# Data work of the gate-and-up and down products taken from GpSimd to VectorE in a hybrid encoder trunk

## The chip, the core and the metric

The kernel runs on one core of one Trainium2 chip. The metric is the device time of one execution in microseconds, of which the median over several executions counts.

## The reference, cut to what matters

The model is an encoder trunk of two layers on 1040 tokens (16 learned tokens ahead of 1024) of width 1024. What the change touches is the second half of each layer, the feed-forward network, and the norm ahead of it:

```python
for l in range(DEPTH):                       # DEPTH = 2
    h = h + hybrid_mixer(rmsnorm(h, norm1_w[l]), ...)   # ends in mix @ w_out
    h = h + swiglu(rmsnorm(h, norm2_w[l]), w_gate_up[l], w_down[l])
h = rmsnorm(h, final_norm_w)

def rmsnorm(x, w):
    y = x * lax.rsqrt(jnp.mean(x * x, axis=-1, keepdims=True) + RMS_EPS)
    return y * w

def swiglu(h, w_gate_up, w_down):            # 1024 -> 2 x 2816 -> 1024
    gate, up = jnp.split(h @ w_gate_up, 2, axis=-1)
    return (jax.nn.silu(gate) * up) @ w_down
```

All data is float32.

## The kernel before, in words

Activations lie transposed: 128 features on the partitions, tokens along the free dimension. Every float32 operand of a product is split into a high part (rounded to the type that TensorE takes, by a copy on ScalarE) and a low part (operand minus high part), and a product is three matmuls: high times high, high times low, low times high. So each weight tile of 128 x 512 costs one copy on ScalarE and one subtraction, and the subtraction is what most of the change moves.

The work of a layer, in order of the parts that matter here:

- **Output projection** (`out_part`, called twice for each of the 8 feature blocks, `z` naming the half of the tokens). Its weights come through `wload` and `wsplit`; their low parts are made on GpSimd (L131) and stay there. After each block, ScalarE squares the new residual (L949) and L950 adds it to the running sum of squares. For `z == 1` and even `m` above 0 that addition is on GpSimd, three times in a layer.
- **Operands of gate and up.** Gate and up are computed together by a scheme of seven products P1 to P7 on 2 x 2 blocks instead of eight (Strassen's idea: blocks of tokens, of input features, and the pair gate/up). The token operands B11, B21, B22, T1 to T4 are sums of normalised blocks, formed on VectorE in L1078, L977, L178 and L965 while the last blocks of the output projection still run. In this stretch the weights A11 and A12 of the first four feature rows are already multiplied (`early_part`, eight calls of `w_op`).
- **Gate and up**, a loop over `f`, 22 rows of 128 features. For each row four weight tiles are loaded (A11, A12, A21, A22), four sums are formed on VectorE (L1290, L1291, L1294, L1295), seven tiles (five for the first four rows) are split by `w_op` (high part L997 on ScalarE, low part L998), and seven products run, in layer 0 in two parts `j` of 260 columns, in layer 1 in one part of 512. VectorE and ScalarE read the products out of PSUM (P5 at L1314, P6 and P3 at L1325 and L1328, P7 at L1332, P4 at L1341; P1 and P2 on ScalarE). P3 is accumulated into the bank of P5, P7 and P4 into the bank of P6, so these products wait until the product before them in their bank has been read out. At the end of a row gate and up are multiplied by the scale of the norm (gate L1355, up L1356), gate goes through SiLU on ScalarE (L1357), and L1358 multiplies the two.
- **Down**, 84 units (`UNITS`) of the same scheme on w_down: `w_unit` splits one weight tile of 128 x 384 (high part L1196, low part L1197), five units ahead of its use; `t_pair` splits the token operand (L1244, L1245). `behind(...)` adds an order dependency on the read-out of two units before.

`tt` is an elementwise operation of two tensors on VectorE, `ptt` the same on GpSimd, `act` an operation on ScalarE. The order of the instructions in each engine's queue is not written out by hand: a scheduler places them by its own cost model, so a change of engine also changes the orders of the queues. Each engine works through its queue in order.

Of the kernel before, what the change touches and what calls it, by code (L numbers as in the profile page):

```python
# [7 lines left out]
F32 = mybir.dt.float32  # L8
# [3 lines left out]
ALU = mybir.AluOpType  # L12
# [30 lines left out]
def trunk(ctx: ExitStack, tc: tile.TileContext, xT, w_in, w_ba, w_out, w_gu, w_dn,  # L43
# [8 lines left out]
    def nm(p):  # L52
        cnt[0] += 1
        return f"{p}_{cnt[0]}"
# [45 lines left out]
    tt = nc.vector.tensor_tensor  # L100
    stt = nc.vector.scalar_tensor_tensor
    ts = nc.vector.tensor_scalar
    ptt = nc.gpsimd.tensor_tensor
# [42 lines left out]
    def dense(ws, xs, chunks, evac, pool=None):  # L146

        for (n0, n1) in chunks:
            n = n1 - n0
            ps = (pool or pacc)()  # L150
            K = len(xs)
            here = tc.cur_priority
            if mmp[0] is not None:
                at_prio(mmp[0])
            for k in range(K):
                (wh, wl), (xh, xl) = ws[k], xs[k]
                mm(ps[:, :n], wh, xh[:, n0:n1], start=(k == 0), stop=False)  # L157
                mm(ps[:, :n], wh, xl[:, n0:n1], start=False, stop=False)  # L158
                mm(ps[:, :n], wl, xh[:, n0:n1], start=False, stop=(k == K - 1))  # L159
            if mmp[0] is not None:  # L160
                mmp[0] = tc.cur_priority
                at_prio(here)
            here = tc.cur_priority
            if evp[0] is not None:
                at_prio(evp[0])
            evac(ps[:, :n], n0, n1)
            if evp[0] is not None:
                evp[0] = tc.cur_priority
                at_prio(here)
            for q in (jobs, jobs2, jobs3):  # L170
                f = q.pop(0) if q else None
                if f is not None:
                    f()
# [106 lines left out]
    for l in range(DEPTH):  # L280
# [660 lines left out]
        def out_part(z, m):  # L941
            dense(wload(w_out[l, m, :, 0:4, :], 4), os_, hcut[z], add_h(m), pwide)

            v, sv = half(hr[m][:, o0:L], z), half(ss[:, o0:L], z)
            if m == 0:
                act(out=sv, in_=v, func=AF.Square)
            else:
                sq = c4k("sq")[:, 0:NB].rearrange("p (g e) -> p g e", g=2)
                act(out=sq, in_=v, func=AF.Square)  # L949
                (ptt if z == 1 and m % 2 == 0 else tt)(out=sv, in0=sv, in1=sq, op=ALU.add)  # L950
            for (n0, n1) in hcut[z]:
                dma(hd[m][:, n0:n1], hr[m][:, n0:n1])

# [39 lines left out]
        def w_op(src, early=False):  # L993
            hi, lo = wslot(early)
            n = src.shape[1]
            hi, lo = hi[:, 0:n, :], lo[:, 0:n, :]
            act(out=hi, in_=src, func=AF.Copy)  # L997
            ptt(out=lo, in0=src, in1=hi.bitcast(F32), op=ALU.subtract)  # L998
            return hi, lo

        bn = [0]
# [116 lines left out]
        def behind(ins):  # L1118

            return after(ins, read_out.get(at[0] - 2))  # L1120
# [58 lines left out]
        def w_unit(u):  # L1179

            p, b, m = UNITS[u]
            n = 4 * b + m
            i = u % 8
            if i in (0, 4, 6):
                hi, lo = (wp.tile([128, WK, 128], F32R, tag=t, name=nm(t)).rearrange("p a b -> p (a b)")[:, 0:384] for t in ("whi", "wlo"))
            else:
                j = {1: 0, 2: 1, 3: 2, 5: 3, 7: 4}[i]
                hi, lo = (dw["W"][:, 384 * (2 * j + q):384 * (2 * j + q) + 384] for q in range(2))
            if p in ("P5", "P6", "P7"):
                r = s_raw(n)  # L1190
            elif p == "P3":
                r = a_raw(0, 1, n)
                behind(tt(out=r, in0=r, in1=s_raw(n), op=ALU.subtract))
            else:
                r = a_raw(*{"P2": (0, 1), "P1": (0, 0), "P4": (1, 1)}[p], n)
            act(out=hi, in_=r, func=AF.Copy)  # L1196
            ptt(out=lo, in0=r, in1=hi.bitcast(F32), op=ALU.subtract)  # L1197
            dw["w", u] = [t.rearrange("p (k e) -> p k e", k=3) for t in (hi, lo)]

        def t_raw(i):  # L1200
# [79 lines left out]
        for f in range(FT):  # L1280
            A11, A12, A21, A22 = raw4("raw"), raw4("raw"), raw4("ck2"), raw4("ck2")
            dma(A11, w_gu[l, f, 0, :, 0:4, :])
            dma(A21, w_gu[l, f, 1, :, 0:4, :])
            dma(A22, w_gu[l, f, 1, :, 4:8, :])
            dma(A12, w_gu[l, f, 0, :, 4:8, :])
            s1t, s2t = raw4("ck2"), raw4("ck2")
            W = {}
            if f >= NE:
                W["A11"] = w_op(A11)
            tt(out=s1t, in0=A21, in1=A22, op=ALU.add)  # L1290
            tt(out=s2t, in0=s1t, in1=A11, op=ALU.subtract)  # L1291
            W["S1"] = w_op(s1t)
            W["S2"] = w_op(s2t)
            tt(out=s2t, in0=A12, in1=s2t, op=ALU.subtract)  # L1294
            tt(out=A21, in0=A11, in1=A21, op=ALU.subtract)  # L1295
            end = f == FT - 1
            for n, a in ([("S3", A21), ("A22", A22), ("S4", s2t), ("A12", A12)] if end else
                         [("S4", s2t), ("S3", A21), ("A12", A12), ("A22", A22)]):
                if f >= NE or n != "A12":
                    W[n] = w_op(a)  # L1300
            adds = s_under(f)
            g, u = early[f] if f < NE else (row((X[1], Y[1])[f % 2] + "f"), row(X[1], F32, 3))
            ps = {}


            def p1(j):
                ps["a", j], ps["c", j], ps["b", j] = pbank(), pbank(), pbank()
                if f >= NE:
                    prod(ps["a", j], W["A11"], T["B11"], j, True)
                    act(out=part(u, 0, j), in_=pin(ps["a", j]), func=AF.Copy)  # L1310

            def p5(j):
                prod(ps["c", j], W["S1"], T["T1"], j, True)
                tt(out=part(u, 1, j), in0=pin(ps["c", j]), in1=part(u, 0, j), op=ALU.add)  # L1314

            def p3(j):
                prod(ps["c", j], W["S4"], T["B22"], j, False)
                (gadd if end else gset)(ps["c", j], j)

            def p6(j):  # L1320
                prod(ps["b", j], W["S2"], T["T2"], j, True)
                (gset if end else gadd)(ps["b", j], j)

            def gset(p, j):
                tt(out=part(g, 1, j), in0=pin(p), in1=part(u, 0, j), op=ALU.add)  # L1325

            def gadd(p, j):
                tt(out=part(g, 1, j), in0=pin(p), in1=part(g, 1, j), op=ALU.add)  # L1328

            def p7(j):  # L1330
                prod(ps["b", j], W["S3"], T["T3"], j, False)
                tt(out=part(u, 1, j), in0=pin(ps["b", j]), in1=part(u, 1, j), op=ALU.add)  # L1332

            def p2(j):
                if f >= NE:
                    prod(ps["a", j], W["A12"], T["B21"], j, False)
                    act(out=part(g, 0, j), in_=pin(ps["a", j]), func=AF.Copy)

            def p4(j):
                prod(ps["b", j], W["A22"], T["T4"], j, False)  # L1340
                tt(out=part(u, 0, j), in0=pin(ps["b", j]), in1=part(u, 0, j), op=ALU.add)  # L1341

            p1_ = (p1, p6, p7)
            if end:

                for p in (p1, p5, p6, p7, p4, p3, p2):
                    for j in range(NJ):
                        p(j)
                    down_begins(p)
            else:  # L1350
                for j in range(NJ):
                    for p in (p1, p5, p3, p6, p7, p2, p4):
                        p(j)
            gv, uv, rv = g[:, o0:L], u[:, o0:L], ss[:, o0:L]
            ptt(out=gv, in0=gv, in1=rv, op=ALU.mult)  # L1355
            tt(out=uv, in0=uv, in1=rv, op=ALU.mult)  # L1356
            act(out=gv, in_=gv, func=AF.Silu)  # L1357
            row_done = tt(out=uv, in0=uv, in1=gv, op=ALU.mult)  # L1358
            for to, r, o in adds:
                after(tt(out=to, in0=r, in1=o, op=ALU.add), row_done if f < FT - 1 else row_before)  # L1360
            row_before = row_done
            dma(ad[f][:, o0:L], uv)
            if NF <= f < NF + NP:
                tt(out=gv[:, 0:NB].rearrange("p (g e) -> p g e", g=2), in0=half(uv, 1), in1=half(uv, 0), op=ALU.subtract)
                dma(td[f - NF], gv[:, 0:NB])
# [45 lines left out]
        for u, (p, b, m) in enumerate(UNITS):  # L1411
            if b == 1 and p in FIRST:
                dh, z = FIRST[p]
# [14 lines left out]
            for j in range(NJ):  # L1428
# [9 lines left out]
                if b == NBK - 1:  # L1438
                    dh, z, op = TO[p]
# [11 lines left out]
        else:  # L1451
# [22 lines left out]
            for (n0, n1) in FIN:  # L1474
                e = (n1 - n0) // 4
                sv = ss[:, n0:n1]
# [6 lines left out]
                for m in range(KT):  # L1483
# [4 lines left out]
                    else:  # L1488
                        summed(sv, True, False)
                        sq = c4k("sq")[:, 0:n1 - n0]  # L1490
# [87 lines left out]
```

## Time and profile before

| | |
|---|---|
| runs | 2550.4, 2552.06, 2552.34 us; median 2552.06 us |
| span of the profiled execution | 2550.9 us |
| TensorE (PE) busy | 2489.1 us, 98% of the span |
| VectorE (DVE) busy | 1636.6 us, 64% |
| GpSimd (POOL) busy | 1135.7 us, 45% |
| ScalarE (ACT) busy | 1045.7 us, 41% |
| mean granted TensorE clock | 0.996 of full speed |

The profile does not state the profiled execution's time apart from its span; the span lies among the three runs, 1.2 us below their median. In rows of the trace, a line such as L998 is a line of the kernel, followed by engine, operation, and written tile <- read tiles. In the table by windows each row is a stretch of the span: its length, then the busy time and number of instructions of each engine, the granted clock and the share and rate of the DMA engines. In the table of waits a row says which engine, tile and line waited for which, the total, the count and the longest wait.

Layer 0 has its output projection until about 625 us, gate and up from there to about 1070 us, and down to 1262 us; layer 1 has the same parts until about 1890, 2325 and 2500 us.

### The profile page before, as it was taken

The page shows a single profiled execution, that of the slowest core. Times are in us where ns is not written, and L with a number is a line of the kernel's source. Part 1 is how long each engine was busy: PE and PEld are TensorE (multiplying, and loading weights), DVE is VectorE, ACT ScalarE, POOL GpSimd, SP SyncE. Part 2 cuts the span into 40 slices and gives each one's busy share as a digit, 9 for nine tenths or more (in the row PEclk, how much of TensorE's full clock was granted, in tenths as well). Part 3 has the DMA queues.
Part 4 walks back from the last instruction along what each step waited for, and adds up shares of the span by engine and source line. Part 5 has one row for each costly group of instructions (what it writes and reads, how often), then busy time and mean ns, then how long its engine had stood idle before and what let it go on. Part 6 is the DMA issues. An engine that isn't in the chain of part 4 may idle for free. (4 is left out here: it accounts for less than half of the span.)

```text
span 2550.9 us, 45282 instructions
## 1 busy us (share of the span) xinstructions
PE 2489.1 (98%) x17508; PEld 2277.7 (89%) x17508; DVE 1636.6 (64%) x2547; ACT 1045.7 (41%) x1944; POOL 1135.7 (45%) x885
## 2 busy tenths in 40 slices
PE   8999999998999999999999999999989999999998
PEld 6989999998999999999999888998968778777787
DVE  4788233749766655767657892335687777558664
ACT  5554333535233333344445543334443333234444
POOL 2131212525666666655411212233557666575662
PEclk9999999999999999999999999999999999999999
DMA  3445253633223322764224443446332233328641
GB/s 129 135 158 169 100 167 125 202 93 119 97 101 103 108 92 85 236 204 136 92 81 144 148 159 108 156 129 201 121 118 91 95 107 103 100 94 273 189 121 66
DMA packets 199531, 335.27 MB, mean 131 GB/s; under 512 B 23404, under 2 KB 85668, under 8 KB 199316
## 3 DMA queue, kind: packets, MB, share of 16 engines
q1 hardware_dynamic: 171204, 293.84, 35.6%
q10 hardware_dynamic: 25936, 34.19, 4.1%
q0 software_dynamic: 2176, 4.36, 0.6%
q8 instruction: 137, 2.24, 0.4%
q14 instruction: 78, 0.64, 0.1%
HBM read 250.31 MB, written 81.99 MB: 130 GB/s over the span
## 5 line engine op out<-in xcount | busy, mean ns | idle before, releaser
L131 POOL TENSOR_TENSOR wlo<-raw,whi 128x512 fp32r<-128x512 f32 x132 | 177.7, 1348 | 661.2 <-ACT whi L130 538.0
L157 PE MATMUL pacc<-a,whi 128*128 128x346 f32 (+1 forms) x808 | 263.7, 329 | 8.0 <-ACT whi L130 7.7
L159 PE MATMUL pacc<-a,wlo 128*128 128x346 f32 (+1 forms) x808 | 262.3, 326 | 0.9 <-DVE wlo L131 0.5
L157 PE MATMUL pacc<-b,whi 128*128 128x346 f32 (+2 forms) x672 | 233.6, 348 | 2.5 <-ACT b L900 1.8
L159 PE MATMUL pacc<-b,wlo 128*128 128x346 f32 (+2 forms) x672 | 232.7, 348 | 0.8 <-DVE wlo L131 0.8
L158 PE MATMUL pacc<-a,whi 128*128 128x346 f32 (+1 forms) x688 | 224.9, 327 | 0.0
L158 PE MATMUL pacc<-b,whi 128*128 128x346 f32 (+2 forms) x580 | 200.3, 345 | 0.0
L130 ACT ACTIVATE whi<-raw 128x512 fp32r<-128x512 f32 x168 | 106.0, 631 | 224.1 <-PE pacc L158 119.0
L998 POOL TENSOR_TENSOR wlo<-rw,whi 128x512 fp32r<-128x512 f32 x92 | 133.8, 1456 | 74.8 <-ACT whi L997 73.5
L157 PEld LDWEIGHTS pacc<-a,whi 128*128 128x128 f32 x808 | 152.2, 189 | 13.8 <-ACT whi L130 8.1
L159 PEld LDWEIGHTS pacc<-a,wlo 128*128 128x128 f32 x808 | 152.6, 189 | 2.0 <-POOL wlo L131 0.7
L157 PEld LDWEIGHTS pacc<-b,whi 128*128 128x128 f32 x672 | 126.5, 188 | 14.4 <-issue 3.1
L159 PEld LDWEIGHTS pacc<-b,wlo 128*128 128x128 f32 x672 | 126.3, 188 | 9.7 <-DVE wlo L131 1.0
L158 PEld LDWEIGHTS pacc<-a,whi 128*128 128x128 f32 x688 | 130.0, 189 | 3.0 <-issue 1.9
L998 POOL TENSOR_TENSOR a<-rw,a 128x512 fp32r<-128x512 f32 x64 | 105.8, 1655 | 57.2 <-ACT a L997 56.2
L998 POOL TENSOR_TENSOR b<-rw,b 128x512 fp32r<-128x512 f32 x64 | 91.1, 1427 | 85.2 <-ACT b L997 59.8
L997 ACT ACTIVATE whi<-rw 128x512 fp32r<-128x512 f32 x92 | 57.8, 630 | 147.0 <-DVE rw L1294 76.7
L158 PEld LDWEIGHTS pacc<-b,whi 128*128 128x128 f32 x580 | 109.2, 188 | 7.0 <-issue 0.4
L997 ACT ACTIVATE b<-rw 128x512 fp32r<-128x512 f32 x64 | 40.1, 630 | 128.6 <-PE pacc L1016 32.3
L1290 DVE TENSOR_TENSOR rw<-rw,rw 128x512 f32<-128x512 f32 x44 | 61.4, 1395 | 45.6 <-POOL wlo L998 25.4
L296 DVE TENSOR_TENSOR a<-pacc,rstd 128x346 f32<-128x346 f32 (+2 forms) x59 | 32.6, 554 | 89.4 <-PE pacc L159 89.1
L998 POOL TENSOR_TENSOR wlo<-raw,whi 128x512 fp32r<-128x512 f32 x50 | 73.3, 1468 | 31.7 <-ACT whi L997 25.1
(967 smaller groups left out, 8439.8 us busy)
## 6 DMA issues: line engine op xcount, KB each, us to landing
raw<-in_w_in SPq DMA_DIRECT2D x112, 256.0 KB, 2.7
raw<-in_w_gu SPq DMA_DIRECT2D x104, 256.0 KB, 2.7
rw<-in_w_gu SPq DMA_DIRECT2D x88, 256.0 KB, 3.1
rw<-in_w_dn SPq DMA_DIRECT2D x94, 192.0 KB, 2.5
rec<-vkd SPq DMA_DIRECT2D x61, 256.0 KB, 2.8
raw<-in_w_out SPq DMA_DIRECT2D x48, 256.0 KB, 2.5
b<-ad SPq DMA_DIRECT2D x45, 260.0 KB, 3.4
a<-ad SPq DMA_DIRECT2D x45, 256.0 KB, 4.1
```

The costliest lines, as they stand in the source:

```text
L130: whi_done[0] = act(out=hi, in_=raw[:, 0:kk, :], func=AF.Copy)
L131: (tt if lov[0] else ptt)(out=lo, in0=raw[:, 0:kk, :], in1=hi.bitcast(F32), op=ALU.subtract)
L157: mm(ps[:, :n], wh, xh[:, n0:n1], start=(k == 0), stop=False)
L158: mm(ps[:, :n], wh, xl[:, n0:n1], start=False, stop=False)
L159: mm(ps[:, :n], wl, xh[:, n0:n1], start=False, stop=(k == K - 1))
L296: tt(out=t[:, n0:n1], in0=ps, in1=rstd[:, n0:n1], op=ALU.mult)
L997: act(out=hi, in_=src, func=AF.Copy)
L998: ptt(out=lo, in0=src, in1=hi.bitcast(F32), op=ALU.subtract)
L1290: tt(out=s1t, in0=A21, in1=A22, op=ALU.add)
```

## The change

Four expressions move from GpSimd to VectorE. No operand, shape or count changes. The low parts of `w_unit` also get the order dependency `behind`.

```diff
@@ out_part: sums of squares, three a layer
-                (ptt if z == 1 and m % 2 == 0 else tt)(out=sv, in0=sv, in1=sq, op=ALU.add)
+                tt(out=sv, in0=sv, in1=sq, op=ALU.add)
@@ w_op: low parts of the gate and up weights
-            ptt(out=lo, in0=src, in1=hi.bitcast(F32), op=ALU.subtract)
+            tt(out=lo, in0=src, in1=hi.bitcast(F32), op=ALU.subtract)
@@ w_unit: low parts of the down weights
-            ptt(out=lo, in0=r, in1=hi.bitcast(F32), op=ALU.subtract)
+            behind(tt(out=lo, in0=r, in1=hi.bitcast(F32), op=ALU.subtract))
@@ end of a row of gate and up: the norm's scale on gate
-            ptt(out=gv, in0=gv, in1=rv, op=ALU.mult)
+            tt(out=gv, in0=gv, in1=rv, op=ALU.mult)
```

`wsplit` (L131), the scale products of the mixer and the last norm's scaling keep their work on GpSimd.

## The prediction, made before the changed kernel ran

> **What bounds the kernel now.** I read the page first, then busy times by stage, then what TensorE waits for in each stage, then the rows of VectorE (DVE) and GpSimd (POOL) side by side at one of these waits.
>
> ```profile
> span 2550.9 us, 45282 instructions
> PE 2489.1 (98%) x17508; PEld 2277.7 (89%) x17508; DVE 1636.6 (64%) x2547; ACT 1045.7 (41%) x1944; POOL 1135.7 (45%) x885
> ```
>
> TensorE is busy for 2489.1 of 2550.9 us. No change on another engine can win more than the 61.8 us that it stands idle, and only the part of it that lies in the stages touched. The table by windows splits the two layers into ramp (last output projection, operands of gate and up), first rows, steady rows, and down:
>
> ```profile
> core 0: us, PE busy (x) PEld busy (x) DVE busy (x) ACT busy (x) POOL busy (x), PEclk, DMA share, GB/s
> 575.00:625.00 50.00, 43.64 (x348) 41.97 (x347) 47.81 (x53) 25.82 (x46) 26.59 (x17) 1.00 0.39 118
> 625.00:700.00 75.00, 70.23 (x569) 67.85 (x568) 58.55 (x72) 22.93 (x37) 52.89 (x30) 1.00 0.30 100
> 700.00:1070.00 370.00, 364.30 (x3010) 361.48 (x3009) 234.04 (x315) 126.63 (x226) 235.75 (x148) 1.00 0.34 112
> 1110.00:1262.00 152.00, 151.79 (x1230) 151.38 (x1229) 100.84 (x145) 66.27 (x124) 78.12 (x62) 1.00 0.45 135
> 1840.00:1890.00 50.00, 42.13 (x246) 35.49 (x245) 46.11 (x51) 24.98 (x39) 24.14 (x16) 0.97 0.36 114
> 1890.00:1965.00 75.00, 71.37 (x295) 56.77 (x294) 55.00 (x50) 24.58 (x38) 54.21 (x33) 0.95 0.32 106
> 1965.00:2325.00 360.00, 354.45 (x1528) 286.11 (x1527) 242.72 (x232) 120.05 (x194) 234.72 (x148) 1.00 0.35 115
> 2345.00:2500.00 155.00, 153.47 (x654) 121.94 (x654) 103.86 (x118) 70.03 (x129) 93.72 (x80) 1.00 0.48 145
> ```
>
> Idle TensorE time is 6.4 and 7.9 us in the ramps, 4.8 and 3.6 us in the first rows, 5.7 and 5.55 us in the steady rows, 0.2 and 1.5 us in down: 35.6 us in all. In the ramps VectorE is busy for 47.81 and 46.11 of 50 us, so there it is the bound; elsewhere TensorE is. What TensorE waits for, first in the steady rows of layer 0, then of layer 1, then the three longest in the ramp and first rows of layer 1:
>
> ```profile
> PE pacc L1015 <- DVE a L1332: 3.6, 9, 0.4
> PE pb L1015 <- DVE a L1332: 0.8, 2, 0.4
> PE pf L1015 <- DVE b L1332: 4.0, 3, 1.8
> PE pacc L157 <- ACT whi L130: 3.4, 1, 3.4
> PE pa L1015 <- DVE a L1328: 3.2, 1, 3.2
> PE pa L207 <- DVE rstd L950: 3.1, 1, 3.1
> ```
>
> Eleven times in layer 0, once in most rows, P4 waits 0.4 us for the read-out of P7 (L1332). The timeline shows one of these, and why; the first three rows are VectorE's, the next two GpSimd's, the last is TensorE's:
>
> ```profile
> 791.28 1.77 DVE L1290 TENSOR_TENSOR rw<-rw,rw 128x512 f32<-128x512 f32 x1 [1.51 <-POOL wlo L998]
> 793.09 2.81 DVE L1295 TENSOR_TENSOR rw<-raw,rw 128x512 f32<-128x512 f32 x1
> 795.82 0.42 DVE L1332 TENSOR_TENSOR a<-pb,a 128x260 f32<-128x260 f32 x1
> ...
> 791.21 1.30 POOL L998 TENSOR_TENSOR wlo<-raw,whi 128x512 fp32r<-128x512 f32 x1
> 792.46 2.89 POOL L1355 TENSOR_TENSOR a3f<-a3f,rstd 128x1040 f32<-128x1040 f32 x1
> ...
> 796.29 0.39 PE L1015 MATMUL pb<-a,a 128*128 128x260 f32 x1 [0.40 <-DVE a L1332]
> ```
>
> L1295 takes 2.81 us, and ends within 0.6 us of the end of GpSimd's L1355, which ran beside it. The same operation on the same shape takes a quarter of that where GpSimd does nothing:
>
> ```profile
> L131 DVE TENSOR_TENSOR wlo<-raw,whi 128x512 fp32r<-128x512 f32 x36 | 24.6, 684 | 2.0 <-ACT whi L130 1.7
> L1295 DVE TENSOR_TENSOR rw<-raw,rw 128x512 f32<-128x512 f32 x44 | 85.2, 1936 | 1.0
> L1290 DVE TENSOR_TENSOR rw<-rw,rw 128x512 f32<-128x512 f32 x44 | 61.4, 1395 | 45.6 <-POOL wlo L998 25.4 <-DMA rw<-in_w_gu 13.3 <-POOL a3f L857 3.3
> L416 DVE TENSOR_TENSOR a<-a,bc 128x1040 f32<-128x1040 f32 x4 | 5.0, 1238 | 1.1 <-DMA bc<-rnd 1.1
> L1325 DVE TENSOR_TENSOR a3f<-pf,a 128x260 f32<-128x260 f32 x9 | 3.9, 428 | 15.4 <-PE pf L1017 15.4
> ```
>
> So a VectorE operation with both inputs in SBUF, 0.684 us alone, averages 1.395 or 1.936 us beside GpSimd: it waits until GpSimd's instruction is over. Read-outs of PSUM keep their 0.43 us (L1325), but stand behind it in the queue.
>
> **The change, part by part.** It moves 526 instructions. The counts and GpSimd's present time, one row each for L998, L1197, L1355 and L950 over the whole span:
>
> ```profile
> 0.00:2551.00 2551.00, 457.77 (x308) 1.00 0.41 131
> 0.00:2551.00 2551.00, 211.01 (x168) 1.00 0.41 131
> 0.00:2551.00 2551.00, 120.38 (x44) 1.00 0.41 131
> 0.00:2551.00 2551.00, 9.29 (x6) 1.00 0.41 131
> ```
>
> GpSimd loses 798.5 us, nearly all that it does in these stages. VectorE gains, by the nearest rows: 308 low parts at 0.684 (L131, the identical operation, 36 times on VectorE already), 210.7 us; 168 of three quarters the size, taken at 0.684 x 3/4 = 0.513, 86.2 us (upper bound 0.684, 114.9 us); 44 scale products at 1.238 (L416, same shape), 54.5 us; 6 sums at 0.684 for nearly the same size, 4.1 us. Sum 355 us. What counts is whether this fits beside TensorE, stage by stage.
>
> *Steady rows.* A row costs TensorE 7 products x 2 parts x 12 matmuls = 168 matmuls at 364.30/3010 = 0.121 us, 20.3 us. VectorE's queue for a row is then 10 read-outs at 0.428 (4.3), four weight sums and seven low parts at 0.684 (7.5), gate scale, up scale and their product at 1.238 (3.7), and two smaller sums bounded by 0.684 each (1.4): 16.9 us, 83% of the row. Even with no relief from GpSimd's absence the stage would hold: with the 18 rows that fit into the window, 234.04 + 18 x (7 x 0.684 + 1.238) = 342.5 of 370 us. So throughput stays with TensorE, and what decides is lateness of a read-out. I walked through one row of the built order of the changed kernel with these durations. P7 of a part has 28 matmuls between its end and the P4 that waits for its read-out, 3.4 us; the read-out stands directly behind instructions of 0.684 us, and ends some 1 us after the product. P3's read-out of P5 and P7's read-out of P6 come out 2.3 us or more ahead of need. The 1.3 to 2.9 us instructions of GpSimd that made L1295 late are gone. So the 0.4 us waits go: 4.4 us in layer 0. In layer 1 the same kind of wait is 4.0 us in three pieces; its evidence is thinner, I take 3. What is late next is a low part itself: it waits in VectorE's queue for ScalarE's high part, and everything queued behind it, read-outs included, waits along; the 2.3 us cover that.
>
> *Ramps.* Here VectorE is the bound, so it must be summed. Four kinds of instruction stand there, in both ramps together 32 of L977, 16 of L965, 8 of L178 and 8 of L1078; below, for each, the sum over the two windows, then one instance that ran free:
>
> ```profile
> sum 100.00, DVE 34.76; mean DVE 17.38
> sum 100.00, DVE 22.52; mean DVE 11.26
> sum 100.00, DVE 12.14; mean DVE 6.07
> sum 100.00, DVE 7.78; mean DVE 3.89
> 592.82 0.75 DVE L977 SCALAR_TENSOR_TENSOR a<-a,npar 128x520 f32<-128x520 f32 x1
> 583.21 1.23 DVE L965 TENSOR_TENSOR b<-a,b 128x1040 fp32r<-128x1040 f32 x1
> 604.52 0.75 DVE L178 SCALAR_TENSOR_TENSOR b<-a,par,b 128x520 fp32r<-128x520 f32 x1
> 576.56 0.49 DVE L1078 TENSOR_SCALAR a<-a,par 128x520 f32<-128x520 f32 x1 [1.31 <-DMA hd<-a]
> ```
>
> The excess over the free durations is 10.8 + 2.8 + 6.1 + 3.9 = 23.6 us. Added are 9 low parts and 3 sums in each ramp, 24 x 0.684 = 16.4 us. Were all contention gone, the ramps would shrink by 7.2 us; but of GpSimd's 17 and 16 instructions in these windows (the table) only 12 move in each; nine of 33, L131, stay, so I keep a quarter of the excess, 5.9 us. Net gain 1.3 us; bounds: 7.2 us gained, and 16.4 us lost if nothing is relieved. For the first rows I add 1.7 us, half of the 3.2 us wait for L1328, which stands behind L1290, an instruction of the stretched kind that also waits for loads; together 3 us.
>
> *Down.* TensorE has 0.2 us idle in layer 0 and 1.5 in layer 1. VectorE would hold 100.84 + 62 x 0.684 = 143.2 of 152 us at most, without any relief. Weights are split five units ahead, so I cost this at nothing; if the cover went, it would be a read-out late by one low part.
>
> *DMA.* No DMA moves, but the weight buffers are now freed by VectorE's low parts instead of GpSimd's. Loads that queue on SP behind them come at most one row's queue later and are prefetched over one row: nothing.
>
> **Sum** against the span of 2550.9 us: -4.4 - 3 - 3 = -10.4 us, so a span of 2540.5. The profile shows no time around the span; the runs' median lies 1.2 us above it, so 2541.7 us (-0.41%).
>
> **The rivals.**
> *The ramps become longer.* VectorE is full there, and 12 instructions are put on it in each. If the stretched durations come from elsewhere than GpSimd, the 16.4 us are lost in full while the steady rows gain nothing: 2552.06 + 16.4 = 2568.5. For it: 47.81 of 50 us. Against: free instances of each kind in the same windows. It decides from the point where less than 16.4 of the 23.6 us is relieved. The Trainium skill ("Perfetto Trace Analysis", Optimizing Scalar/DVE Operations) advises to take work off a saturated VectorE, even to GpSimd, which read alone speaks against this change in the ramps; its next sentence warns that the two engines share an SBUF port and that such a move might not help, with which the rows above agree.
> *The queue blocks.* Low parts wait for ScalarE's high part, which waits for TensorE to release a weight buffer; before, that wait stood harmlessly on GpSimd. If a read-out comes behind one such wait in every row beyond its 2.3 us, one low part's 0.684 us is added to each of 44 rows: +30 us, 2582. For it: the built order has low parts ahead of read-outs in each row. Against: the walk.
> *Nothing.* Other waits of like size replace those of 0.4 us, since VectorE now runs at 83% of a row: 2552.
>
> **How the numbers follow.** Forecast 0.55, ramps 0.13, blocked queue 0.12, nothing 0.20. About 0.2% (5 us) is what a measurement of this kernel can tell from no change. Forecast's tail into no change and nothing's tail into a gain about cancel: faster 0.56, same 0.20, slower 0.24. The low end takes all steady idle (11.2 us) and half of the 22.7 us of ramps and first rows: 2529.5, rounded to 2529. The high end includes the ramp rival: 2569. Left out are the blocked queue and a little below, under 2 in 10.
>
> **What would show it.** Right: L1290 and L1295 at 0.7 us mean; VectorE's busy time up by much less than the 355 us added; no 0.4 us waits of P4 for L1332. Wrong: waits of TensorE for L1314 to L1341 longer than before in the windows of gate and up (blocked queue), or ramps with more idle TensorE time than 6.4 and 7.9 us while L977 is short (ramp rival).

## The result, and the profile after

The changed kernel takes 2516.9 us (median of four runs, 2513.0 to 2517.4), the kernel before 2552.2 us (four runs, 2550.4 to 2552.8). The ratio is 0.9867, with a 95% interval of 0.9854 to 0.9880: a gain of 35 us, where 10.4 were forecast, and below the low end of the range. The page of the kernel after:

```profile
span 2515.4 us, 44862 instructions
PE 2478.2 (99%) x17508; PEld 2276.9 (91%) x17508; DVE 1696.9 (67%) x3073; ACT 1045.9 (42%) x1944; POOL 340.0 (14%) x359
```

VectorE took over 526 instructions, worth 355 us by their free durations, and is busy for only 60.3 us more (1696.9 against 1636.6): the other 295 us were time in which its instructions stood still beside GpSimd. TensorE issues the same 17508 matmuls, and its busy time fell by 10.9 us all the same; this comes up again below. The table by windows, with some windows shortened and those of layer 1 moved forward because the stages begin earlier (columns as in the prediction's table):

```profile
core 0: us, PE busy (x) PEld busy (x) DVE busy (x) ACT busy (x) POOL busy (x), PEclk, DMA share, GB/s
575.00:625.00 50.00, 47.27 (x392) 46.30 (x391) 46.23 (x71) 28.97 (x52) 7.49 (x5) 1.00 0.41 132
625.00:700.00 75.00, 74.80 (x628) 74.35 (x621) 64.81 (x112) 25.71 (x41) 0.00 (x0) 1.00 0.32 112
700.00:1050.00 350.00, 350.00 (x2920) 350.00 (x2919) 266.25 (x448) 120.06 (x218) 0.00 (x0) 1.00 0.34 112
1100.00:1250.00 150.00, 150.00 (x1205) 150.00 (x1205) 104.51 (x197) 67.28 (x124) 8.73 (x7) 1.00 0.41 128
1825.00:1875.00 50.00, 46.91 (x254) 38.71 (x254) 47.18 (x70) 28.68 (x45) 5.05 (x3) 0.97 0.36 117
1875.00:1950.00 75.00, 74.31 (x321) 59.88 (x320) 61.13 (x88) 25.20 (x37) 0.00 (x0) 1.00 0.32 111
1950.00:2270.00 320.00, 320.00 (x1382) 259.08 (x1381) 233.80 (x338) 106.16 (x172) 0.00 (x0) 1.00 0.32 108
2300.00:2450.00 150.00, 146.40 (x622) 117.44 (x621) 110.86 (x193) 70.04 (x129) 10.65 (x13) 0.99 0.53 162
```

In the steady rows of both layers TensorE has no idle time at all, and VectorE does its larger work at 76% and 73% of the window. The ramps keep 2.7 and 3.1 us of idle TensorE time, and VectorE is as full there as before. The groups of VectorE's instructions, over the whole span:

```profile
L1290 DVE TENSOR_TENSOR rw<-rw,rw 128x512 f32<-128x512 f32 x44 | 32.3, 734 | 10.7 <-DMA rw<-in_w_gu 6.1 <-POOL a3f L857 3.3 <-POOL b3f L857 0.6
L1295 DVE TENSOR_TENSOR rw<-raw,rw 128x512 f32<-128x512 f32 x44 | 30.1, 685 | 0.1
L998 DVE TENSOR_TENSOR wlo<-rw,whi 128x512 fp32r<-128x512 f32 x92 | 62.8, 686 | 4.8 <-ACT whi L997 4.1
L1355 DVE TENSOR_TENSOR b3f<-b3f,rstd 128x1040 f32<-128x1040 f32 (+1 forms) x19 | 23.3, 1227 | 0.0
L1197 DVE TENSOR_TENSOR wlo<-rw,whi 128x384 fp32r<-128x384 f32 x26 | 14.3, 555 | 4.4 <-ACT whi L1196 4.4
```

Weight sums are back at their free 0.68 to 0.73 us, and the moved instructions cost nearly what the prediction took: 686 ns, 1227 ns and 555 ns (taken: 684, 1238, 513). The stretch of VectorE around the P4 that waited before, in one row of layer 0:

```profile
777.62 0.69 DVE L1290 TENSOR_TENSOR rw<-rw,rw 128x512 f32<-128x512 f32 x1
778.23 0.69 DVE L998 TENSOR_TENSOR wlo<-raw,whi 128x512 fp32r<-128x512 f32 x1
778.84 1.24 DVE L1355 TENSOR_TENSOR a3f<-a3f,rstd 128x1040 f32<-128x1040 f32 x1
779.99 0.69 DVE L1295 TENSOR_TENSOR rw<-raw,rw 128x512 f32<-128x512 f32 x1
780.59 0.42 DVE L1341 TENSOR_TENSOR a<-pb,a 128x260 f32<-128x260 f32 x1
781.02 0.43 DVE L1332 TENSOR_TENSOR a<-pb,a 128x260 f32<-128x260 f32 x1
```

Before, L1290 and L1295 alone took 4.6 us here; now these two, a low part and the scale product take 3.1 us from the first start to the last end, and the read-out L1332 that P4 needs comes in time.

**Time by stage.** Windows that are moved by hand don't show where 35 us went. Each trace holds 17508 matmuls in nearly the same order, so the start of the k-th marks the same amount of TensorE's work in every kernel. I cut the span at the matmuls 4650, 5550, 8250 and 10050 for layer 0 and 14400, 14850, 16350 and 17250 for layer 1, and took the differences of the start times:

| us, both layers | ramps and first rows | further rows | down | all else |
|---|---|---|---|---|
| before | 229.5 | 685.4 | 436.4 | 1186.8 |
| after, against before | -22.9 | -13.8 | -0.3 | +1.8 |

The two layers share alike: -11.7 and -11.2 in the ramps and first rows, -7.6 and -6.2 in the rows. The same differences are given below for each experiment. Each stage figure comes from one profiled execution. "All else" has no edit in it but for the last three kernels below, and moves by up to 2 us from one kernel to the next without one, down by up to 5; differences of that size there are not read.

The granted TensorE clock is part of these figures too. It falls to half for 3.4 us or 6.8 us at a time; in the rows of layer 1 some 4.3 matmuls start in a us, and in such a stretch 2.3 or fewer. In the ramps and first rows, between these matmuls, the trace of the kernel before has 10.2 us at half clock, all in layer 1 (granted clock 0.97 and 0.95 in the prediction's table), that of the changed kernel 3.4 us (0.97 and 1.00 above). Up to 3.4 of the 11.2 us of layer 1 may therefore be the clock; layer 0, at full clock there in both kernels, gained 11.7 us without it. The traces of the experiments have 0 to 13.7 us at half clock in these stages, one of them 23.9; where it bears on a difference, the text says so. Whether TensorE's pauses bring these drops about, no run tests.

### The profile page after: what moved, and what is told of

Its sections match the earlier page's. It is cut to its first block, busy times and chain, and to the rows that moved or that the text cites. A ratio compares the mean times of both kernels' runs of the same rounds, so it can differ in the third digit from the quotient of the medians.

```text
span 2515.4 us, 44862 instructions
## 1 busy us (share of the span) xinstructions
PE 2478.2 (99%) x17508; PEld 2276.9 (91%) x17508; DVE 1696.9 (67%) x3073; ACT 1045.9 (42%) x1944; POOL 340.0 (14%) x359
## 5 line engine op out<-in xcount | busy, mean ns | idle before, releaser
L131 POOL TENSOR_TENSOR wlo<-raw,whi 128x512 fp32r<-128x512 f32 x132 | 176.4, 1338 | 1285.4 <-ACT whi L130 1116.7
L296 DVE TENSOR_TENSOR b<-pacc,rstd 128x346 f32<-128x346 f32 (+1 forms) x63 | 32.5, 516 | 82.8 <-PE pacc L159 82.8
L131 POOL TENSOR_TENSOR a<-raw,a 128x512 fp32r<-128x512 f32 x3 | 3.9, 1285 | 597.1 <-ACT a L130 597.1
L997 ACT ACTIVATE a<-rw 128x512 fp32r<-128x512 f32 x64 | 40.0, 629 | 101.7 <-PE pacc L1016 60.3
L998 DVE TENSOR_TENSOR wlo<-rw,whi 128x512 fp32r<-128x512 f32 x92 | 62.8, 686 | 4.8 <-ACT whi L997 4.1
L1015 PE MATMUL pacc<-b,whi 128*128 128x260 f32 (+1 forms) x172 | 53.5, 311 | 0.7 <-ACT b L1051 0.7
```

The costliest lines, as they stand in the source:

```text
L131: (tt if lov[0] else ptt)(out=lo, in0=raw[:, 0:kk, :], in1=hi.bitcast(F32), op=ALU.subtract)
L296: tt(out=t[:, n0:n1], in0=ps, in1=rstd[:, n0:n1], op=ALU.mult)
L1015: mm(ps[:, :CW], w[0][:, k, :], th[:, cs], start=first and k == 0, stop=False, skip_group_check=True)
```

## The experiments

All are made from the changed kernel unless it is said otherwise. "Back" means that the line issues on GpSimd again. Each time is a median of four runs, or of five where noted; before is the kernel before in runs on the same chip (medians of 2549.8 to 2552.2 us). Not all rounds ran on the same chip, so between kernels the ratios compare better than the times.

**One edit back.**

```diff
-            tt(out=lo, in0=src, in1=hi.bitcast(F32), op=ALU.subtract)      # L998
+            ptt(out=lo, in0=src, in1=hi.bitcast(F32), op=ALU.subtract)
```

> The changed kernel with the 308 low parts of L998 back on GpSimd; the other three edits stay. Contention theory (an operation of VectorE with two SBUF inputs is held up while GpSimd works, and the gain comes from the end of that): GpSimd has 458 us of its 799 us again, all in gate and up and in the ramps, so nearly all of the 35 us comes back: 2540 to 2550 us, L977, L965 and L1294 stretched again in the ramps. Rival, scale product (the gain hangs on L1355, whose 2.9 us held L1295 up): at most 12 us come back: 2517 to 2529 us.

```diff
-            tt(out=gv, in0=gv, in1=rv, op=ALU.mult)                        # L1355
+            ptt(out=gv, in0=gv, in1=rv, op=ALU.mult)
```

> The changed kernel with the 44 scale products of L1355 back on GpSimd; the low parts stay on VectorE. The prediction's account of the steady rows (L1295 is held up by L1355, so that P7's read-out is late for P4): the 0.4 us waits of P4 for L1332 come back in most rows, 12 us in all by what the steady rows gained: 2527 to 2530 us. Rival (with the low parts off GpSimd nothing is near enough to the limit for one 2.4 us instruction a row to matter): no wait comes back, 2515 to 2519 us.

```diff
-            behind(tt(out=lo, in0=r, in1=hi.bitcast(F32), op=ALU.subtract))  # L1197
+            ptt(out=lo, in0=r, in1=hi.bitcast(F32), op=ALU.subtract)
```

> The changed kernel with the 168 low parts of down (L1197) back on GpSimd and without their order behind the read-outs. TensorE is idle for 0.2 and 1.5 us in down, so contention theory and prediction both say no change: 2515 to 2519 us, though L1197 stretches VectorE's operations there by some 55 us in all. Rival (the low part's place matters, a new order of the units of down): over 2 us either way.

```diff
-                tt(out=sv, in0=sv, in1=sq, op=ALU.add)                     # L950
+                (ptt if z == 1 and m % 2 == 0 else tt)(out=sv, in0=sv, in1=sq, op=ALU.add)
```

> The changed kernel with only the six sums of squares of L950 back on GpSimd. With L998 and L1355 both put back, the ramps and first rows still kept 9 us of their 23 us gain, so something else of the change carries these. Theory chain (the sums stand on the chain output projection, sum, scale row, L207; on GpSimd each takes 1.5 us and waits behind a weight's low part, and TensorE waited 3.1 us for L950): 4 to 9 us come back, all in the ramps: 2520 to 2526 us. Rival, quiet GpSimd (with the low parts gone from its queue a sum on GpSimd is no later than on VectorE): 2515 to 2519 us.

| kernel | us | ratio to before, 95% | ramps, first rows | rows | down |
|---|---|---|---|---|---|
| after | 2516.9 | 0.9867 (0.9854-0.9880) | -22.9 | -13.8 | -0.3 |
| L998 back | 2523.9 | 0.9892 (0.9874-0.9910) | -11.3 | -13.8 | -5.3 |
| L1355 back | 2521.3 | 0.9877 (0.9857-0.9897) | -15.8 | -12.9 | -1.5 |
| L1197 back | 2519.7 | 0.9881 (0.9855-0.9907) | -22.7 | -13.8 | +1.5 |
| L950 back | 2519.8 | 0.9879 (0.9863-0.9894) | -20.5 | -13.9 | +1.5 |

My expectation for L998 fell: it has 458 of the 799 us that left GpSimd, and putting it back costs 7 us, not 23 to 33. L1355 fell between its two expectations: the rows keep nearly all of their gain (no wait came back), but the ramps and first rows lose 7.1 us, of which up to 3.4 may be the clock (10.2 us at half clock, as with L998 back). L1197 does nothing that can be told from no change, as forecast. The four losses add up to 7.0 + 4.4 + 2.8 + 2.9 = 17 us of 35: the edits don't add. The intervals of the last three overlap with that of the changed kernel, so of these only the stage figures speak.

**Two edits back.** L998 and L1355 together, by the first two of the diffs above.

> The changed kernel with L998 (308 low parts) and L1355 (44 scale products) both back on GpSimd; down's low parts and the sums of squares stay on VectorE. Put back alone they cost 7 and 4 us. Theory two together (a read-out of P7 is late only when GpSimd's queue holds low parts and the long scale product back to back beside VectorE's weight sums, and either one on VectorE ends that): the 0.4 us waits of P4 for L1332 are back in most rows, each costing 0.67 us by the distance of the matmuls' starts, 14 us in all, and the ramps are long again: 2543 to 2551 us. Rival, each by itself (the costs of the two add up, and the rest of the 35 us lies in the other two edits): 2526 to 2531 us.

2540.1 us, 0.9951 (0.9933-0.9969), 3 us below the range of the first theory: ramps and first rows -9.1, rows -0.4. The rows have lost all of their gain, which neither edit cost alone. The waits of TensorE in the rows of layer 0 of this kernel, 700 to 1050 us (for what it waited, us in all, times, longest), answer to those of before:

```profile
PE pacc L1015 <- DVE a L1332: 3.2, 8, 0.4
PE pb L1015 <- DVE a L1332: 0.9, 2, 0.5
```

In the kernel after this view is empty. So the wait needs both on GpSimd. From the side of before, with only the scale product moved:

```diff
-            ptt(out=gv, in0=gv, in1=rv, op=ALU.mult)
+            tt(out=gv, in0=gv, in1=rv, op=ALU.mult)
```

> The kernel before with only L1355's 44 scale products moved to VectorE. Theory either one (the late read-out needs the long scale product as well as the low parts on GpSimd): the steady rows win all of their 13.8 us, the ramps what L1355 cost there, 2 to 7 us: 2531 to 2538 us. Rival (the low parts alone keep the read-outs late, since 458 us of GpSimd's work stay): steady rows within 2 us of before, 2546 to 2552 us.

2538.7 us, 0.9954 (0.9939-0.9969): rows -13.9, ramps and first rows -5.7, of which up to 3.4 may be the clock. All of the rows' gain, with 308 low parts still on GpSimd.

**The same work in shorter instructions.** The kernel before, with one edit; no work changes its engine.

```diff
-            ptt(out=gv, in0=gv, in1=rv, op=ALU.mult)
+            [ptt(out=gv[:, E*i:E*i+E], in0=gv[:, E*i:E*i+E], in1=rv[:, E*i:E*i+E], op=ALU.mult) for i in range(4)]
```

> The kernel before, all work where it was, with the scale product of L1355 issued on GpSimd as four instructions of 260 columns in place of one of 1040. GpSimd does the same work, if anything some more time of it. Theory length (an operation of VectorE waits for the end of the GpSimd instruction that runs, so it is the 2.7 us of one instruction that make L1295 and the read-out behind it late): L1295 falls from 1.94 towards 1.2 us, the 0.4 us waits of the steady rows go, 7 and 6 us there: 2534 to 2543 us. Rival, amount (what counts is how long GpSimd works beside VectorE in a row): no change, 2548 to 2555 us.

2541.5 us (five runs), 0.9968 (0.9955-0.9981). Rows -13.9 us by the trace of its fastest run: the whole gain of the rows, with GpSimd doing all that it did. Its groups of L1355 in the kernel before, then in this one, and the two weight sums of VectorE in this one:

```profile
L1355 POOL TENSOR_TENSOR b3f<-b3f,rstd 128x1040 f32<-128x1040 f32 (+1 forms) x19 | 53.3, 2804 | 4.5 <-DVE b3f L1328 3.3 <-ACT b3f L1337 1.2
```

```profile
L1355 POOL TENSOR_TENSOR b3f<-b3f,rstd 128x260 f32<-128x260 f32 (+1 forms) x76 | 75.0, 1002 | 16.9 <-DVE b3f L1328 9.8 <-ACT b3f L1337 7.0
...
L1290 DVE TENSOR_TENSOR rw<-rw,rw 128x512 f32<-128x512 f32 x44 | 58.4, 1326 | 50.4 <-POOL wlo L998 28.3 <-DMA rw<-in_w_gu 10.4 <-POOL b L998 7.9
L1295 DVE TENSOR_TENSOR rw<-raw,rw 128x512 f32<-128x512 f32 x44 | 50.5, 1148 | 1.0
```

GpSimd needs more time for it (75.0 us instead of 53.3 in this group), and still L1295 falls from 1936 to 1148 ns. One steady row of layer 0 in this kernel, first VectorE, then GpSimd:

```profile
787.40 1.78 DVE L1290 TENSOR_TENSOR rw<-rw,rw 128x512 f32<-128x512 f32 x1 [1.51 <-POOL wlo L998]
789.21 1.13 DVE L1295 TENSOR_TENSOR rw<-raw,rw 128x512 f32<-128x512 f32 x1
790.26 0.41 DVE L1332 TENSOR_TENSOR a<-pb,a 128x260 f32<-128x260 f32 x1
...
787.34 1.29 POOL L998 TENSOR_TENSOR wlo<-raw,whi 128x512 fp32r<-128x512 f32 x1
788.59 1.20 POOL L1355 TENSOR_TENSOR a3f<-a3f,rstd 128x260 f32<-128x260 f32 x1
```

VectorE's order is that of the waiting row before (L1290, L1295, L1332), so another order on VectorE does not explain it. What counts in the rows is how long one GpSimd instruction lasts, not how much GpSimd works. With that, the results above fit one account, in which L1290 and L1295 stand ahead of the read-out that P4 needs. In most steady rows of layer 0 the two lasted 1.77 + 2.81 = 4.58 us before, and P4 waited 0.40 us; they may then last some 4.2 us, an estimate, since other instructions can stand between them. With both edits back they take 4.58 us again: waits. With L998 back alone they take 1.77 + 0.68 = 2.45, with L1355 back alone 0.69 + 2.94 = 3.63, with the split 1.78 + 1.13 = 2.91: no waits. Over the ramps and first rows the split gains only 0.4 us, in a trace that has 23.9 us at half clock there against 10.2 before.

**GpSimd busy to no use.** The changed kernel, with GpSimd's old work done again into tiles that are dead, so that all results still come from VectorE:

```diff
-            w = w_op(A, True)
+            w = w_op(A, True); ptt(out=A, in0=A, in1=w[0].bitcast(F32), op=ALU.subtract)
...
-            W["S1"] = w_op(s1t)
+            W["S1"] = w_op(s1t); ptt(out=s1t, in0=s1t, in1=W["S1"][0].bitcast(F32), op=ALU.subtract)
...
-                    W[n] = w_op(a)
+                    W[n] = w_op(a); ptt(out=a, in0=a, in1=W[n][0].bitcast(F32), op=ALU.subtract)
...
             row_done = tt(out=uv, in0=uv, in1=gv, op=ALU.mult)
+            if not NF <= f < NF + NP: ptt(out=gv, in0=gv, in1=rv, op=ALU.mult)
```

> The changed kernel, with GpSimd doing again, to no use, what it did before: behind the low parts of the early parts and of S1, S4, S3, A12 and A22 (five of seven in a row) the same subtraction of the same size into the raw weights, which are dead by then, and behind the row's last product a scale product of the same size as L1355 into the dead gate row, though not in rows 4 to 12 of a layer. All results still come from VectorE. Theory contention: the rows with both get the 0.4 us waits for L1332 again, rows 4 to 12 don't, and the ramps lose what L998 cost there: 2528 to 2542 us. Rival, latency (low part and scale product are ready earlier on VectorE, and that is the gain): 2515 to 2519 us.

2574.8 us, 1.0090 (1.0075-1.0105): worse than before by 23 us and than after by 58, more than expected. Against before: ramps and first rows +8.9, rows +9.4 (up to 3.4 of these the clock, in layer 1). The rows hold their own control, since rows 4 to 12 have no idle scale product. A window inside those rows, and one inside the later rows, both of layer 0:

```profile
740.00:900.00 160.00, 160.00 (x1338) 160.00 (x1338) 146.43 (x206) 53.27 (x96) 62.37 (x40) 1.00 0.33 106
920.00:1040.00 120.00, 115.26 (x944) 113.54 (x944) 110.19 (x139) 36.57 (x69) 61.55 (x34) 1.00 0.24 80
```

TensorE has no idle time where GpSimd runs five low parts a row, and 4.7 us in 120 where a scale product of 2.55 us is added to them. That product gives nobody a result, so a result that comes earlier from VectorE is not needed to explain a loss in the rows. It is not the same wait as before, though, as the longest waits of the second window show: mostly TensorE waits for the read-out of P5 (L1314), not for L1332.

```profile
PE pf L1015 <- DVE a L1314: 1.9, 2, 1.0
PE pa L1015 <- DVE a L1314: 1.7, 2, 0.9
PE pf L1015 <- DVE a L1332: 0.4, 1, 0.4
```

In the ramps and first rows the useless work costs 31.8 us against after (22.9 + 8.9), up to 5.1 of these the clock; there the raw weights are also held until it is done, as they were before.

An earlier try, five short additions behind each low part:

```diff
+            [ptt(out=scr, in0=lo[:, k % n, 0:96].bitcast(F32), in1=lo[:, k % n, 0:96].bitcast(F32), op=ALU.add) for k in range(5)]
```

> The changed kernel, and behind each low part of L998 five additions on GpSimd, each of 96 columns of that low part into a scratch tile that nobody reads: GpSimd works beside VectorE for about as long as with L998 on it, while every result still comes from VectorE and the order on the other engines stays nearly as it is. Contention theory: operations of VectorE with SBUF inputs are stretched again and the time goes back most of the way: 2535 to 2550 us. Rival, latency (the gain is that a low part is there after 0.684 us on VectorE instead of 1.3 us and a queue on GpSimd, so that TensorE gets its weights earlier): no change, 2515 to 2520 us. Rival, order (the gain is the other order in which the engines' work was laid out): no change either, 2515 to 2520 us.

2637.3 us, 1.0333 (1.0314-1.0353), and no test of the question: the load was far too large. GpSimd, with 1540 additions of 0.57 us, was busy for 307.8 of 350 us in the rows, and VectorE waited 74.5 us there for it to let go of low parts that it was about to overwrite. One row of it does speak, though:

```profile
L1295 DVE TENSOR_TENSOR rw<-raw,rw 128x512 f32<-128x512 f32 x44 | 35.1, 798 | 0.1
```

Beside a GpSimd that is busy for 88% of the time, but with instructions of 0.57 us, L1295 is stretched to only 0.80 us.

**What VectorE's added work costs.** The low parts of L998 left out:

```diff
-            tt(out=lo, in0=src, in1=hi.bitcast(F32), op=ALU.subtract)
-            return hi, lo
+            return hi, hi
```

> The changed kernel with the 308 low parts of L998 left out: the products use the high part twice, so part of the computation is changed. GpSimd is as quiet as in the changed kernel, and VectorE has 211 us less to do. Theory hidden (what was put on VectorE lies beside other work, the ramps too): 2513 to 2518 us. Rival, VectorE-bound ramps (the step of the prediction that charged every added instruction of the ramps in full, 18 low parts of 0.684 us there): 2503 to 2506 us.

2508.0 us, 0.9833 (0.9818-0.9848), between the two expectations; its products use the high part twice, so it computes something else. Only 3.3 us of the difference to after lie in the ramps and first rows (-26.2 instead of -22.9), and 0.3 in the rows; the rest is in down and in stages where L998 does not occur. So 211 us of added low parts cost 3 to 4 us. Over the ramps and first rows VectorE is busy for 38 us less than in the changed kernel (147.6 instead of 185.6 us), and these stages are only 3.3 us shorter.

**Which part of the ramps.** Only the 16 low parts of the early parts back:

```diff
-            tt(out=lo, in0=src, in1=hi.bitcast(F32), op=ALU.subtract)
+            (ptt if early else tt)(out=lo, in0=src, in1=hi.bitcast(F32), op=ALU.subtract)
```

> The changed kernel with only the 16 low parts of the early parts (8 in each layer's ramp) back on GpSimd. Theory ramp (what L998 costs on GpSimd, it costs in the ramps by stretching L977, L965, L178 and L1078): about as much as L998 alone, 5 to 8 us: 2522 to 2526 us, L965 and L977 stretched. Rival, first rows (it is the low parts of the rows behind the ramp that cost): under 2 us: 2515 to 2519 us.

2522.8 us, 0.9892 (0.9875-0.9908): ramps and first rows -15.1. These 16 low parts carry 7.8 of the 11.6 us that L998 carries there, as the ramp theory had it; up to 1.7 of the one and 3.4 of the other may be the clock. And the sums alone, in the kernel before:

```diff
-                (ptt if z == 1 and m % 2 == 0 else tt)(out=sv, in0=sv, in1=sq, op=ALU.add)
+                tt(out=sv, in0=sv, in1=sq, op=ALU.add)
```

> The kernel before with only the six sums of L950 moved to VectorE; all else of the change left out. Theory chain: the 9 us of the ramps that did not hang on L998 and L1355 are the sums': 2542 to 2547 us, the wait of L207 for L950 gone. Rival (they hang on a joint effect of the four edits, or on the order of down): 2550 to 2554 us.

2539.7 us, 0.9958 (0.9943-0.9972), below both expectations: ramps and first rows -8.2, so six instructions of 1.5 us do carry some 8 us while the low parts are on GpSimd, though only 2.4 when they aren't (the kernel with L950 back). But the reason that I gave is wrong. TensorE's wait for L950 in the ramp of layer 1 has not gone in this kernel; it was 3.1 us:

```profile
PE pa L207 <- DVE rstd L950: 3.7, 1, 3.7
```

**Going on.** The output projection's low parts to VectorE too, then L929 as well, and, apart from these, all low parts of L131 everywhere.

```diff
+        lov[0] = True          # ahead of the output projection's loop
...
+        lov[0] = False         # behind the last early part
```

> The changed kernel, going on: the low parts of the output projection's weights (L131 from the output projection to the last early part, some 24 a layer on GpSimd) go to VectorE too, so that GpSimd does nothing in the ramps. Theory contention: what is left of the stretch (L977 at 0.91 us instead of 0.75) goes, up to 4 us won in the ramps: 2512 to 2516 us. Rival, full VectorE (it is busy for 46 to 47 of 50 us in the ramps, and each low part is now added in full there): 2518 to 2526 us.

```diff
-                (tt if n0 == o0 else ptt)(out=ol[:, h, n0:n1], ...)
+                tt(out=ol[:, h, n0:n1], ...)
```

> The best version so far (the changed kernel with the output projection's low parts on VectorE as well), and L929 too, the attention output's low parts of the inner columns (24 on GpSimd), so that GpSimd has nothing left between attention and down. Theory contention: what still stretches VectorE at the start of the output projection goes: 2 to 4 us more, 2504 to 2507 us. Rival (TensorE waits there for these low parts, and on VectorE they come one behind the other instead of side by side): 2509 to 2514 us.

```diff
-        (tt if lov[0] else ptt)(out=lo, in0=raw[:, 0:kk, :], ...)
+        tt(out=lo, in0=raw[:, 0:kk, :], ...)
```

> The changed kernel with all 138 remaining low parts of L131 on VectorE, in attention too, where other work stays on GpSimd (L716, L729, L857). Theory, always better on VectorE: another gain of some us: 2505 to 2514 us. Rival, dependent on the stage (VectorE is over 80% busy there in parts of the span, and weights' low parts stand ahead of read-outs that TensorE waits for): slower, 2520 to 2540 us.

| kernel | us | ratio to before, 95% | ramps, first rows | rows | all else |
|---|---|---|---|---|---|
| output projection too | 2508.6 | 0.9828 (0.9811-0.9844) | -28.6 | -13.8 | -2.0 |
| and L929 | 2510.2 | 0.9841 (0.9825-0.9858) | -28.0 | -13.8 | -2.0 |
| all of L131 | 2511.7 | 0.9845 (0.9826-0.9863) | -28.2 | -13.8 | +6.0 |

The first beats both kernels and both of its expectations: 8 us below after, 5.7 of them in the ramps and first rows (up to 1.7 of these the clock, which stays full there). The windows of layer 0 now have 0.8 us idle TensorE time, with GpSimd silent:

```profile
575.00:625.00 50.00, 49.17 (x404) 47.65 (x403) 47.19 (x77) 30.59 (x54) 0.00 (x0) 1.00 0.43 132
625.00:700.00 75.00, 75.00 (x628) 75.00 (x627) 62.57 (x111) 23.94 (x37) 0.00 (x0) 1.00 0.33 108
```

L929 adds nothing. All of L131 gains the same in the ramps and gives time back ahead of the first ramp, where projections and attention stand: 7.0 us more than before there, 5.3 more than after, by the trace of its slowest run.

## Why the prediction was right or wrong

**The bound of the whole and the mechanism: right.** TensorE bounds the kernel, VectorE is held up while a GpSimd instruction runs, and read-outs queue behind it. All three signs named for this came: L1290 and L1295 at 734 and 685 ns, VectorE's busy time up by 60 instead of 355 us, no wait of P4 for L1332. The split shows the mechanism without moving any work. The Trainium skill ("SBUF — State Buffer", Who interferes with whom) states that a VectorE instruction with two SBUF inputs contends with a GpSimd instruction that reads SBUF, over a shared port that is an exclusive lock, and that one with a single SBUF input, outside its two-port modes, does not contend; the runs agree: 1936 ns beside instructions of 2.8 us, 1148 beside those of 1.0 us, 685 beside none, and 0.42 us for the PSUM read-outs in every kernel.

**Steady rows: right in kind, -13.8 where -7.4 was forecast.** Two terms were too small. Each wait was priced at its visible 0.40 us. From one steady row of layer 0 to the next, 168 matmuls, lay 20.81 us before where P4 waited, and 20.13 to 20.15 us (median) in the kernels without the wait: each wait cost 0.67 us. The gap shows 0.40 of it. Of the other 0.27 us, 0.16 stand in the matmul ahead of the gap, drawn at 0.28 us where otherwise the next one starts after 0.12, and 0.11 behind the gap, where the second matmul starts 0.23 us after the first instead of 0.12. And for layer 1 I took 3 us from one group of 4.0; the windows had 5.55 us idle, and 6.2 were won. The account itself was incomplete: it laid L1295's lateness to L1355 and the other long GpSimd instructions together, and did not see that moving either L1355 or L998 alone ends the wait.

**Ramps and first rows: this step failed, -22.9 where -3.0 was forecast.** The step is "Here VectorE is the bound, so it must be summed": the net of VectorE's busy time, 17.7 us of relief less 16.4 us of added work, was taken for what the ramps would gain. The sum itself came out nearly right. Of the 23.6 us of excess some 5 are left, all in L977 (32 instances, 29.2 us, against 24.0 free), where the prediction kept 5.9; and over the ramps and first rows, between the same matmuls, VectorE is busy for 185.6 us instead of 189.5. But these 3.9 us less went with 22.9 us less of stage, and the 38 us less without the low parts with only 3.3 more. So VectorE's busy sum does not set the length of these stages, though it fills 46 to 47 of 50 us. What sets it hangs on what stands on GpSimd: put back alone, L998 costs 11.6 us there, L1355 7.1 and L950 2.4, up to 3.4 of each of the first two perhaps the clock. That they act by stretching single VectorE instructions on which TensorE's operands wait fits the rows below, but is argued: GpSimd instructions without use cost 31.8 us there, yet they also held the raw weights, and no run settles by which wait it reaches TensorE. L965, L178 and L1078 are at 1.23, 0.75 and 0.48 us in the ramp of layer 0 after the change, and only part of L977 is still stretched, by the L131 that stayed:

```profile
L977 DVE SCALAR_TENSOR_TENSOR a<-a,par,a 128x520 f32<-128x520 f32 x8 | 6.9, 878 | 0.0
...
L965 DVE TENSOR_TENSOR P<-a,P 128x1040 fp32r<-128x1040 f32 x4 | 4.9, 1235 | 0.4 <-ACT P L964 0.4
L977 DVE SCALAR_TENSOR_TENSOR a<-a,npar 128x520 f32<-128x520 f32 x4 | 4.7, 1185 | 0.0
...
L977 DVE SCALAR_TENSOR_TENSOR a<-a,par 128x520 f32<-128x520 f32 x4 | 3.0, 751 | 0.0
L178 DVE SCALAR_TENSOR_TENSOR b<-a,par,b 128x520 fp32r<-128x520 f32 x4 | 3.0, 748 | 0.0
...
L1078 DVE TENSOR_SCALAR a<-a,par 128x520 f32<-128x520 f32 x4 | 1.9, 479 | 1.0 <-DMA hd<-a 1.0
```

The first rows, to which I gave 1.7 us, had the same kind of stretched instructions, which I had looked at only in the ramps. L1291 over ramp and first rows of layer 0, before and after:

```profile
L1291 DVE TENSOR_TENSOR rw<-rw,raw 128x512 f32<-128x512 f32 x6 | 10.7, 1790 | 0.0
```

```profile
L1291 DVE TENSOR_TENSOR rw<-rw,raw 128x512 f32<-128x512 f32 x6 | 4.1, 685 | 0.0
```

The sums of L950, costed at 4.1 us of VectorE's time and no gain, carry 2.4 to 8.2 us, depending on what else is on GpSimd. Why so much, no run settles: the wait that I held responsible stayed when they alone were moved, and the order of VectorE's and TensorE's work differs somewhat between these kernels.

**Down and DMA: right.** L1197 on either engine changes down by less than its spread, and TensorE waits for no load in the stages touched.

**The ceiling.** The idle time of the touched windows, 35.6 us, served as the most that could be won. Ramps and rows together won 36.7 us, and 6.7 us of idle time are still there. Between the same matmuls, visible idle time fell from 32.6 to 6.7 us, by 25.9; the other 10.8 us came out of time that was drawn as busy (10.9 us over the whole span). Up to 3.4 of these may be the clock, which was lower in layer 1 before. The Trainium skill ("Perfetto Trace Analysis", Tensor Engine Instruction) says that a matmul's end in a profile is estimated rather than observed; the 0.27 us of each wait that no gap shows agree with it. With half of the ramps' and first rows' idle time as its low end, the range could not hold the result.

**The rivals.** None came. Longer ramps: with the first rows they are 22.9 us shorter. The advice of the Trainium skill ("Perfetto Trace Analysis", Optimizing Scalar/DVE Operations) to take work off a saturated VectorE, even to GpSimd, would have lost these, while its warning about the shared port held. Blocked queue and "nothing": TensorE waits for no read-out in the rows.

## What to carry to other kernels

Where two engines exclude one another, as VectorE and GpSimd do here, an engine's busy time counts waiting as work: before adding work to a full engine, set each instruction's duration against its free one. Even a right sum of busy time isn't the length of a stage, though: leave work out and see whether the stage gets shorter. In the steady rows a long instruction on GpSimd did the harm, and cutting it into pieces helped as much as giving it to VectorE. Price a TensorE wait by the distance of the same matmuls in rows with and without it, not by the gap in the profile, and find the joint effects of several edits by putting them back in pairs, for single ones can all look small.

## What was not expected of the hardware

- The same scale product in four instructions took GpSimd 75.0 us instead of 53.3 in its largest group, and TensorE's steady rows came out 13.9 us shorter.
- A wait of 0.40 us in the trace of TensorE cost 0.67 us.
- VectorE's weight sums hardly notice a GpSimd that is busy for 88% of the time with instructions of 0.57 us (L1295 at 798 ns).
